# A hybrid SSD and stick-breaking trunk on one core: attention's products written in two parts, the output projection's units three steps earlier, and one sum of squares in PSUM

## The chip, the cores and the metric

The kernel runs on one core of one Trainium2 chip. The core's engines work side by side and meet over semaphores: PE (TensorE, matrix products), DVE (VectorE), ACT (ScalarE), POOL (GpSimd) and SP (SyncE, which here only issues transfers; ACT issues some too). Matmuls read SBUF and write PSUM, which the kernel divides into eight banks of 512 floats a partition. Each engine's instructions run in the order in which they stand, and so do the transfers that one engine issues: an instruction that waits holds all that stand behind it on its engine.

The metric is the device time of one execution in microseconds. Before the change it is 2861.54 us, the median of 3 runs (2855.9 to 2861.61).

## The reference

A trunk of two layers over 1040 tokens (16 learned ones and 1024 from the input), model width 1024, all in float32. Layer 0 is a Mamba-2 mixer and a gated FFN with a causal convolution; layer 1 is stick-breaking attention and such an FFN; RMSNorm stands before each. The parts that the change touches:

```python
def _rmsnorm(x, g):
    y = x * lax.rsqrt(jnp.mean(x * x, axis=-1, keepdims=True) + NORM_EPS)
    return y * g

def _stick_breaking_attention(q, k, v):            # per block of queries
    logits = jnp.einsum('bthd,bshd->bhts', q, k) * scale
    log_keep = jnp.where(visible, jax.nn.log_sigmoid(-logits), 0.0)
    later = lax.cumsum(log_keep, axis=3, reverse=True) - log_keep
    log_w = jnp.where(visible, jax.nn.log_sigmoid(logits) + later, -jnp.inf)
    return jnp.einsum('bhts,bshd->bthd', jnp.exp(log_w), v)

o = _stick_breaking_attention(q, k_shared, v_shared)   # 16 heads of 64
h = h + o @ sb_w_o[j]
h = h + _conv_ffn(_rmsnorm(h, ffn_norm), ...)
```

## The kernel before, in words

**Products.** A float32 product is made of three matmuls on rounded parts: each operand is split into a high part (a copy, by ACT) and a low part (the operand less its high part, by DVE or POOL), and `mm3` (L206 to L211) issues high by high (L209), high weight by low data (L210) and low weight by high data (L211). Where both parts of an operand come from, and when, is what the change moves.

**Attention** (`attention`, L1714). Heads go in 8 pairs. A pair has 18 steps: `i` runs over 9 blocks of 116 queries (the last has 112), `jj` over the thirds of the keys (348, 348, 344) that a block can see, from its own backwards. A step calls `weigh` (logits `lg` on PE, L1651; two sigmoids on ACT, L1652 and L1653; masks on POOL, L1657; two scans and a product on DVE, L1662 and L1663), then `place` and a piece of some projection (`pj` on PE), and `flush(LAG)`, which handles the step two back: `turn` transposes its weights on PE (L1685, `wT`) and ACT copies them out (`wt`, L1691); when a visit's blocks are all there (visits are blocks 0 to 2, 3 to 5, 6 and 7, and 8) the next `flush` calls `values`, PE's products with v (L1708, `po`, one PSUM bank), which ACT copies to `o` (L1710). After blocks 2, 5 and 8 an ACT transfer stores a third of the pair's `o` in DRAM (`o_d`, L1712).

The order of PE, DVE, ACT and POOL in this stage is the order of the program text; the transfers on SP and all other stages are placed by a scheduler.

**The output projection.** In pairs 0 to 6 PE's spare room in a step goes to projections of the next pair; in the last pair it goes to units of `o @ w_o` for pairs 0 to 3 (`o_blocks`, L1805), a generator that is advanced once in each step from `BEHIND` on, twice in each of the four turns of the loop behind the steps (the drain), and to its end in `o_proj`. A unit is 12 matmuls (4 pairs by 3) for 128 rows of output by 256 or 258 tokens, and an add to `h` on DVE (`accumulate`, L528 to L538); there are 8 x 4 of them. Its inputs are fetched by `fetch_o` (one float32 row of 514 or 512 tokens), split by `split_o` (ACT L1802, DVE L1803), and met by weights, which `parts` splits (ACT L1820, POOL through L102). Units write to the pool `mm`, which has two PSUM banks; the logits have two more (`lg2`), the transposes three (`sm`), `po` one (`ex`). Before, the generator's stages are: step 9 loads, steps 10 and 11 split the first two tiles, step 12 is the first unit, step 17 the sixth. Eight more units run in the drain and 18 behind it. Pairs 4 to 7 follow in `o_proj` and `enter_ffn`, with weights `w` from `load_wd`, tile by tile (four tiles of 256 or 258 tokens).

**The norm of the FFN.** Behind the last unit of a row of a tile, `square_row` (L1058) has ACT square it (L1061). For tile 0 (`m` = 8) DVE adds the eight squares up in a running sum (L1063, both operands in SBUF) and one matmul with ones sums over the partitions (L1041); for the other tiles each row has a matmul (L1067). This happens in both layers.

Of the kernel before, what the change touches and what calls it, by code (L numbers as in the profile page):

```python
# [13 lines left out]
P = 128  # L14
# [48 lines left out]
NPOOL = 3  # L63
DT0 = 0
LAG = 2
BEHIND = 9
VISITS = (0, 1, 2), (3, 4, 5), (6, 7), (8,)

NW = 8
# [36 lines left out]
class Trunk:  # L106
# [950 lines left out]

    def square_row(self, ms, h, f, s0, n, m):  # L1058

        q = self.tmp("sq")[:, :n]  # L1060
        self.nc.scalar.activation(q, h[f][:, HB + s0 : HB + s0 + n], AF.Square)  # L1061
        if f % m:
            self.nc.vector.tensor_tensor(self.squares, self.squares, q, op=ALU.add)  # L1063
# [629 lines left out]
    def values(self, p, visit, wt, v, o, od):  # L1693


        nc = self.nc
        first, last = visit[0], visit[-1]
        j, c0 = first // 3, first % 3 * CB
        end = CH[last][0] + CH[last][1]
        n = end - CH[first][0]  # L1700
        each = wt[0][0].shape[1]
        po = self.ex("po")
        order = [*range(first, last + 1), *range(first - 1, -1, -1)]
        for x, c in enumerate(order):
            t0 = max(c - first, 0) * CB
            q, r = divmod(c, each)
            for a in range(2):
                nc.tensor.matmul(po[64 * a : 64 * a + 64, t0:n], v[: CH[c][1], c, 64 * a : 64 * a + 64], wt[a][q][: CH[c][1], r, t0:n],  # L1708
                                 start=x == 0, stop=x == last, skip_group_check=True)
        nc.scalar.activation(o[:, c0 : c0 + n], po[:, :n], AF.Copy)  # L1710
        if last % 3 == 2:
            nc.scalar.dma_start(od[p, :, TT[j][0] : end], o[:, : TT[j][1]])  # L1712

    def attention(self, u, pool, hd):  # L1714


        od = self.dp.tile([PAIRS, P, L], F32, tag="o_d", name="o_d")
# [7 lines left out]
        pairs = [self.heads(u, p, pool) for p in range(PAIRS)]  # L1725
        turns, ready, wts, os, late, chores = [], [], {}, {}, [], []
        behind = self.o_blocks(hd, od)

        def flush(n):
            while ready:  # L1730
                p, visit = ready.pop()
                if visit[0] % 3 == 0:
                    os[p] = self.tmp("o")
# [21 lines left out]
        for p in range(PAIRS):  # L1755
            prev = None
            for n, (i, jj) in enumerate(steps):
# [22 lines left out]
                        chores += pair.load(loads[own, n])  # L1780
                flush(LAG)
                turns.append((p, i, jj, bt))
        while turns or ready:
            next(behind)
            next(behind)
            flush(0)
        return od, behind

    def fetch_o(self, od, p, x):
# [6 lines left out]
        self.nc.sync.dma_start(lo.bitcast(F32), od[p, :, g.at + s0 : g.at + s0 + m])  # L1796
        return hi, lo

    def split_o(self, hl):

        hi, lo = hl
        self.nc.scalar.activation(hi, lo.bitcast(F32), AF.Copy)  # L1802
        self.nc.vector.tensor_tensor(lo, lo.bitcast(F32), hi.bitcast(F32), op=ALU.subtract)  # L1803

    def o_blocks(self, hd, od):  # L1805

# [20 lines left out]

        def unit(f, j):
            w = ws[f]
            self.accumulate(h, f, *g.span(j), lambda i, f: tuple(x[:, i * P : i * P + P] for x in w), rows[j // 2], HB, self.mm, g.part(j // 2)[0])  # L1830
# [24 lines left out]
        for hl in rows[1][2:]:  # L1855
            self.split_o(hl)
        unit(1, 1)
        fetch_w(2)
        fetch_h(2)
        yield  # L1860
        order = [(0, 2), (0, 3), (1, 2), (1, 3)] + [(f, j) for f in range(2, KD) for j in range(4)]
        for x, (f, j) in enumerate(order):
            if x % 4 == 2 and x // 4 + 2 < KD:
                parts(x // 4 + 2)
                if x // 4 + 3 < KD:
                    fetch_w(x // 4 + 3)
                    fetch_h(x // 4 + 3)
            unit(f, j)
            yield

    def o_proj(self, od, blocks, pool):


        a = self.a
        first = PAIRS // 2
        for _ in blocks:
            pass

        def part(p, x):
            hl = self.fetch_o(od, p, x)  # L1880
            self.split_o(hl)
            return hl

        ops = [part(p, 0) for p in range(first, PAIRS)]
        ws = [self.load_wd(a["w_o"][first + i], i < 2) for i in range(4)]
        second = [part(p, 1) for p in range(first, PAIRS)]
        return self.enter_ffn(1, self.ho, [(ws, lambda: ops), (ws, lambda: second)], pool)


# [173 lines left out]
```

## Time and profile before

| | |
|---|---|
| median of 3 timed runs | 2861.54 us |
| profiled execution | 2864.79 us |
| its span, first to last instruction | 2862.9 us |
| mean granted TensorE clock | 0.996 |
| instructions | 56393 |
| attention, pairs 0 to 6 (span's clock) | about 1560 to 2006 us |
| last pair and drain | about 2006 to 2078 us |
| tile 0's squares in layer 1 | 2111 to 2124 us |

An execution has the name of its engine, line, operation and tiles in every row, and times count from the span's start. "x24" is 24 instructions, and an arrow in brackets names how long the engine stood idle before the row and what ended it. In rows of windows, each engine's busy time within the window is followed by its instructions, then come the clock granted to PE (1.00 is full), the busy share of the 16 transfer engines and their rate.

### The profile page before, as it was taken

The page shows a single profiled execution, that of the slowest core. Times are in us where ns is not written, and L with a number is a line of the kernel's source. Part 1 is how long each engine was busy: PE and PEld are TensorE (multiplying, and loading weights), DVE is VectorE, ACT ScalarE, POOL GpSimd, SP SyncE. Part 2 cuts the span into 40 slices and gives each one's busy share as a digit, 9 for nine tenths or more (in the row PEclk, how much of TensorE's full clock was granted, in tenths as well). Part 3 has the DMA queues.
Part 4 walks back from the last instruction along what each step waited for, and adds up shares of the span by engine and source line. Part 5 has one row for each costly group of instructions (what it writes and reads, how often), then busy time and mean ns, then how long its engine had stood idle before and what let it go on. Part 6 is the DMA issues. An engine that isn't in the chain of part 4 may idle for free.

```text
span 2862.9 us, 56393 instructions
## 1 busy us (share of the span) xinstructions
PE 2813.9 (98%) x21251; PEld 2695.1 (94%) x21251; DVE 2073.6 (72%) x3920; ACT 1589.3 (56%) x3093; POOL 1577.6 (55%) x2144
## 2 busy tenths in 40 slices
PE   8999999999999999999999999999899999999998
PEld 7989999999999999999999999999799999999888
DVE  5676666668597666677886888878669776766776
ACT  5555454543265656555335777777636555555433
POOL 2366455643529888868853111122254888885881
PEclk9999999999999999999999999999999999999999
DMA  4343334333413222245132222221432222225331
GB/s 119 88 112 103 107 86 134 108 132 101 126 59 97 81 79 79 80 156 174 43 128 77 66 69 62 63 59 47 136 107 76 80 80 78 81 82 184 111 104 67
DMA packets 136237, 273.32 MB, mean 95 GB/s; under 512 B 15924, under 2 KB 68285, under 8 KB 135965
## 3 DMA queue, kind: packets, MB, share of 16 engines
q1 hardware_dynamic: 130340, 258.55, 28.9%
q0 software_dynamic: 2048, 6.49, 0.6%
q10 hardware_dynamic: 3576, 4.67, 0.5%
q8 instruction: 168, 2.75, 0.4%
q14 instruction: 105, 0.85, 0.1%
HBM read 203.58 MB, written 51.16 MB: 89 GB/s over the span
## 4 chain that ended last, share of the span: by engine, by line
PE 89%; DVE 5%; ACT 2%; issue 2%; POOL 1%; DMA 0%; DVEq 0%; SPq 0%; ACTq 0%; POOLq 0%
PE p L211 10%; PE p L209 10%; PE p L210 10%; PE acc L209 8%; PE acc L211 8%; PE acc L210 8%; PE pj L209 8%; PE pj L210 7%; PE pj L211 7%; PE po L1708 2%; PE lg L1651 2%; PE wT L1685 2%; PE y L810 1%; PE S L799 1%; PE y L812 1%
## 5 line engine op out<-in xcount | busy, mean ns | idle before, releaser
L102 POOL TENSOR_TENSOR wl<-w,wh 128x256 fp32r<-128x256 f32 x760 | 678.9, 923 | 359.8 <-ACT wh L196 216.8
L209 PE MATMUL pj<-uh,wh 128*128 128x348 f32 (+2 forms) x1536 | 500.7, 327 | 2.1 <-DVE xbc L339 1.4
L210 PE MATMUL pj<-ul,wh 128*128 128x348 f32 (+2 forms) x1536 | 494.8, 322 | 0.8 <-DVE ul L320 0.8
L211 PE MATMUL pj<-uh,wl 128*128 128x348 f32 (+2 forms) x1536 | 492.1, 320 | 0.0
L209 PE MATMUL p<-bh,fh 128*128 128x262 f32 (+1 forms) x1408 | 400.8, 285 | 3.9 <-DVE p L1235 3.7
L211 PE MATMUL p<-bh,fl 128*128 128x262 f32 (+1 forms) x1408 | 400.8, 285 | 2.0 <-POOL fl L102 2.0
L210 PE MATMUL p<-bl,fh 128*128 128x262 f32 (+1 forms) x1408 | 397.5, 283 | 0.0
L102 POOL TENSOR_TENSOR fl<-x,fh 128x256 fp32r<-128x256 f32 x352 | 263.9, 782 | 190.3 <-ACT fh L1172 140.0
L210 PE MATMUL p<-bl,wh 128*128 128x262 f32 (+1 forms) x1040 | 295.5, 284 | 0.7 <-DVE bl L1096 0.7
L209 PE MATMUL p<-bh,wh 128*128 128x262 f32 (+1 forms) x1040 | 295.2, 284 | 0.8 <-ACT ft L1232 0.8
L211 PE MATMUL p<-bh,wl 128*128 128x262 f32 (+1 forms) x1040 | 294.3, 283 | 0.0
L209 PEld LDWEIGHTS pj<-uh,wh 128*128 128x128 f32 x1536 | 288.7, 188 | 4.5 <-ACT xbc L336 1.7
L210 PEld LDWEIGHTS pj<-ul,wh 128*128 128x128 f32 x1536 | 289.3, 188 | 2.4 <-DVE ul L320 1.4
L339 DVE SCALAR_TENSOR_TENSOR c<-p,params,c 128x260 f32<-128x260 f32 (+1 forms) x528 | 248.2, 479 | 57.5 <-ACT c L336 50.9
L211 PEld LDWEIGHTS pj<-uh,wl 128*128 128x128 f32 x1536 | 288.7, 188 | 0.1
L209 PEld LDWEIGHTS p<-bh,fh 128*128 128x128 f32 x1408 | 267.8, 190 | 4.8 <-DVE p L1235 4.1
L211 PEld LDWEIGHTS p<-bh,fl 128*128 128x128 f32 x1408 | 265.9, 189 | 2.9 <-POOL fl L102 2.7
L210 PEld LDWEIGHTS p<-bl,fh 128*128 128x128 f32 x1408 | 267.4, 190 | 0.1
L1232 ACT ACTIVATE ft<-p 128x262 f32<-128x262 f32 (+1 forms) x352 | 133.2, 382 | 178.9 <-DVE p L1235 110.9
L210 PE MATMUL acc<-gl,wh 128*128 128x260 f32 (+1 forms) x672 | 214.1, 320 | 0.0
L211 PE MATMUL acc<-gh,wl 128*128 128x260 f32 (+1 forms) x672 | 213.4, 320 | 0.0
L209 PE MATMUL acc<-gh,wh 128*128 128x260 f32 (+1 forms) x672 | 210.7, 320 | 0.1
(337 smaller groups left out, 7712.8 us busy)
## 6 DMA issues: line engine op xcount, KB each, us to landing
w<-in_w_up SPq DMA_DIRECT2D x88, 512.0 KB
w<-in_w_down SPq DMA_DIRECT2D x44, 512.0 KB
w<-in_w_in SPq DMA_DIRECT2D x40, 512.0 KB
E<-ea_d SPq DMA_DIRECT2D x32, 464.0 KB
D<-acs_d SPq DMA_DIRECT2D x32, 420.5 KB
g<-c SPq DMA_DIRECT2D x88, 130.0 KB
g<-c SPq DMA_DIRECT2D x88, 128.0 KB
b<-g SPq DMA_DIRECT2D x16, 520.0 KB
```

The source lines that it names most:

```text
L102: done.append(eng.tensor_tensor(out[:, c], x[:, c], y[:, c], op=op))
L209: self.behind(mm(out, wh, uh, start=first, stop=False, skip_group_check=joins), tie, "behind the sums of squares")
L210: mm(out, wh, ul, start=False, stop=False, skip_group_check=joins)
L211: self.last_mm = mm(out, wl, uh, start=False, stop=last, skip_group_check=joins)
L339: ins = nc.vector.scalar_tensor_tensor(out, ps[:, o + i : o + i + n], wcol(i), out, op0=ALU.mult, op1=ALU.add)
L799: nc.tensor.matmul(ps, bk[:n], xde[:n].rearrange("p h d -> p (h d)"), start=True, stop=True)
L810: nc.tensor.matmul(y, xdt[:n, i, :], dk[:, i, :], start=True, stop=c == 0)
L812: nc.tensor.matmul(y, state[:, i, :], ce[:, i, :], start=False, stop=True)
L1232: nc.scalar.activation(s[:, :N], ps[:, :N], AF.Copy)
L1651: nc.tensor.matmul(ps[:nt, a, :m], part[:, c0 : c0 + nt], ks[a][:, s0 : s0 + m], start=x == 0, stop=x == 1)
L1685: nc.tensor.transpose(pt[:ns, x * CB : x * CB + nt], bt[:nt, a, x * CB : x * CB + ns], self.ident[:nt, :nt])
L1708: nc.tensor.matmul(po[64 * a : 64 * a + 64, t0:n], v[: CH[c][1], c, 64 * a : 64 * a + 64], wt[a][q][: CH[c][1], r, t0:n], start=x == 0, st ...
```

## The change

`values` writes the products as two tiles, `hi` (ACT's copy, now rounded to the high part) and `lo` (a new DVE subtract, L1714 in the changed text, from the same PSUM bank). Both are stored, in a DRAM tile twice as large: high parts by ACT's queue as before, low parts by SP's. `fetch_o` loads both parts with one transfer, so `split_o` is gone (16 copies on ACT, 16 subtracts on DVE). The generator starts at step 5 (`BEHIND`): loads in step 5, weight parts in steps 6 and 7, `h` in step 8, and a unit in each step from 9 on; nine units are done by step 17, and 15 are left behind the drain. Weight blocks are fetched and split one block further ahead. The first two units in the drain take the two banks that the logits had, all others `mm`. For tile 0 of the norm the running sum lies in a PSUM tile of `sm`; the eighth add writes an SBUF tile for the matmul.

```diff
-BEHIND = 9
+BEHIND = 5
...
     def square_row(self, ms, h, f, s0, n, m):
-        q = self.tmp("sq")[:, :n]
+        q = self.sm("sq")[:, :n] if m > 1 and f == 0 else self.tmp("sq")[:, :n]
         self.nc.scalar.activation(q, h[f][:, HB + s0 : HB + s0 + n], AF.Square)
-        if f % m:
-            self.nc.vector.tensor_tensor(self.squares, self.squares, q, op=ALU.add)
-        elif m > 1:
+        if m > 1:
+            if f:
+                out = q if f == m - 1 else self.squares
+                self.nc.vector.tensor_tensor(out, self.squares, q, op=ALU.add)
+                q = out
             self.squares = q
...
-        nc.scalar.activation(o[:, c0 : c0 + n], po[:, :n], AF.Copy)
+        hi, lo = (x[:, c0 : c0 + n] for x in o)
+        nc.scalar.activation(hi.bitcast(F32R), po[:, :n], AF.Copy)
+        nc.vector.tensor_tensor(lo.bitcast(F32R), po[:, :n], hi, op=ALU.subtract)
         if last % 3 == 2:
-            nc.scalar.dma_start(od[p, :, TT[j][0] : end], o[:, : TT[j][1]])
+            for x, (q, t) in enumerate(zip((nc.scalar, nc.sync), o)):
+                q.dma_start(od[p, x, :, TT[j][0] : end], t[:, : TT[j][1]])
...
+        both = self.lg2("acc")
+        banks = iter([lambda s, a=a: both[:, a] for a in range(2)])
+        self.unit_bank = lambda s: next(banks, self.mm)(s)
         while turns or ready:
...
-        hi, lo = t[:, :m], t[:, QW // 2 : QW // 2 + m]
-        self.nc.sync.dma_start(lo.bitcast(F32), od[p, :, g.at + s0 : g.at + s0 + m])
-        return hi, lo
-    def split_o(self, hl):
-        hi, lo = hl
-        self.nc.scalar.activation(hi, lo.bitcast(F32), AF.Copy)
-        self.nc.vector.tensor_tensor(lo, lo.bitcast(F32), hi.bitcast(F32), op=ALU.subtract)
+        both = t.rearrange("p (y c) -> p y c", y=2)[:, :, :m]
+        self.nc.sync.dma_start(both.bitcast(F32), od[p, :, :, g.at + s0 : g.at + s0 + m].rearrange("y p c -> p y c"))
+        return both[:, 0], both[:, 1]
...
         fetch_w(1)
         yield
-        for hl in rows[0][:2]:
-            self.split_o(hl)
-        yield
-        for hl in rows[0][2:]:
-            self.split_o(hl)
         parts(0)
         yield
-        rows[1] = [self.fetch_o(od, p, 1) for p in range(K)]
+        parts(1)
+        fetch_w(2)
+        yield
         fetch_h(0)
         fetch_h(1)
+        yield
+        rows[1] = [self.fetch_o(od, p, 1) for p in range(K)]
+        fetch_h(2)
         unit(0, 0)
         yield
-        parts(1)
         unit(0, 1)
         yield
-        for hl in rows[1][:2]:
-            self.split_o(hl)
         unit(1, 0)
         yield
-        for hl in rows[1][2:]:
-            self.split_o(hl)
         unit(1, 1)
-        fetch_w(2)
-        fetch_h(2)
+        parts(2)
+        fetch_w(3)
+        fetch_h(3)
```

In what follows each row is a place in an engine's order: its line, operation, written tile, read tiles and shape. The line numbers of the changed text are two to five higher than before.

On PE, the last pair's step 9 as it was (logits 116 wide, a projection's half `pj`, then at once step 10's transposes):

```order
L1651 MATMUL lg_24943<-k_23929,qs_24791 116x116 x2
L1616 MATMUL pv_24957<-ident,v_24900 116x128 x3
L209 MATMUL pj_24925<-uh_17766,wh_24228 128x344
L210 MATMUL pj_24925<-ul_17767,wh_24228 128x344
L211 MATMUL pj_24925<-uh_17766,wl_24229 128x344
L209 MATMUL pj_24925<-uh_17768,wh_24228 128x344
L210 MATMUL pj_24925<-ul_17769,wh_24228 128x344
L211 MATMUL pj_24925<-uh_17768,wl_24229 128x344
L1685 MATMUL wT_24980<-ident,bt_24839 116x116 x3
```

And now: the first unit's 12 matmuls (five are shown) stand between that half and step 10's transposes.

```order
L211 MATMUL pj_25022<-uh_17768,wl_24292 128x344
L209 MATMUL acc_25079<-o_24898,wh_24939 128x258
L210 MATMUL acc_25079<-o_24898,wh_24939 128x258
L211 MATMUL acc_25079<-o_24898,wl_24940 128x258
L209 MATMUL acc_25079<-o_24900,wh_24939 128x258
L210 MATMUL acc_25079<-o_24900,wh_24939 128x258
```

On DVE, steps 10 to 12 of the last pair as they were, with scans and product of each step and four splits:

```order
L1662 SCALAR_TENSOR_TENSOR kp_24990<-kp_24990,kp_24940,one 116x349 x2
L1663 TENSOR_TENSOR bt_24991<-bt_24991,kp_24990 116x2x348
L1803 TENSOR_TENSOR o_24968<-o_24968 128x514
L1803 TENSOR_TENSOR o_24970<-o_24970 128x514
L1662 SCALAR_TENSOR_TENSOR kp_25023<-kp_25023,kp_24990,one 116x349 x2
L1663 TENSOR_TENSOR bt_25024<-bt_25024,kp_25023 116x2x348
L1803 TENSOR_TENSOR o_24972<-o_24972 128x514
L1803 TENSOR_TENSOR o_24974<-o_24974 128x514
L1662 SCALAR_TENSOR_TENSOR kp_25063<-kp_25063,one 116x233 x2
```

And now: the splits' places hold the units' adds, and the new subtract (`o` from `po`) stands behind step 12's product, ahead of step 13's scans.

```order
L538 TENSOR_TENSOR h_25029<-h_25029,acc_25079 128x258
L1664 SCALAR_TENSOR_TENSOR kp_25103<-kp_25103,kp_25041,one 116x349 x2
L1665 TENSOR_TENSOR bt_25104<-bt_25104,kp_25103 116x2x348
L538 TENSOR_TENSOR h_25029<-h_25029,acc_25122 128x256
L1664 SCALAR_TENSOR_TENSOR kp_25146<-kp_25146,kp_25103,one 116x349 x2
L1665 TENSOR_TENSOR bt_25147<-bt_25147,kp_25146 116x2x348
L538 TENSOR_TENSOR h_25031<-h_25031,acc_25167 128x258
L1664 SCALAR_TENSOR_TENSOR kp_25191<-kp_25191,one 116x233 x2
L1665 TENSOR_TENSOR bt_25192<-bt_25192,kp_25191 116x2x232
L538 TENSOR_TENSOR h_25031<-h_25031,acc_25208 128x256
L1714 TENSOR_TENSOR o_25232<-po_25233,o_25231 128x348
L1664 SCALAR_TENSOR_TENSOR kp_25260<-kp_25260,kp_25191,one 116x349 x2
```

On SP's queue, around the last pair's loads of o, now: a low part's store (L1717) stands ahead of them and another behind, and the last loads of queries (`qs`), which stood ahead of the loads of o before, stand behind the first four.

```order
L1592 DMA k_23988<-klo_24763 64x344
L1717 DMA o_d<-o_24653 128x344
L1805 DMA o_24898<-o_d 128x2x514
L1805 DMA o_24900<-o_d 128x2x514
L1805 DMA o_24902<-o_d 128x2x514
L1805 DMA o_24904<-o_d 128x2x514
L1607 DMA qs_24859<-qs_24859 64x2x344
L1607 DMA qs_24861<-qs_24861 64x2x344
L1717 DMA o_d<-o_24945 128x348
L1818 DMA w_3489_25227<-in_w_o_f 128x512
L1829 DMA h_25029<-h_d 128x1026
```

More of the change, by code (lines that the diff above doesn't have):

```diff
@@ L1727, in attention @@
         behind = self.o_blocks(hd, od)
+        self.unit_bank = self.mm
         def flush(n):
@@ L1829, in unit @@
             w = ws[f]
-            self.accumulate(h, f, *g.span(j), lambda i, f: tuple(x[:, i * P : i * P + P] for x in w), rows[j // 2], HB, self.mm, g.part(j // 2)[0])
+            self.accumulate(h, f, *g.span(j), lambda i, f: tuple(x[:, i * P : i * P + P] for x in w), rows[j // 2], HB, self.unit_bank, g.part(j // 2)[0])
         rows[0] = [self.fetch_o(od, p, 0) for p in range(K)]
@@ L1875, in o_proj @@
         first = PAIRS // 2
+        self.unit_bank = self.mm
         for _ in blocks:
             pass
[L1879 to L1884, printed above, removed]
+        ops = [self.fetch_o(od, p, 0) for p in range(first, PAIRS)]
         ws = [self.load_wd(a["w_o"][first + i], i < 2) for i in range(4)]
-        second = [part(p, 1) for p in range(first, PAIRS)]
+        second = [self.fetch_o(od, p, 1) for p in range(first, PAIRS)]
         return self.enter_ffn(1, self.ho, [(ws, lambda: ops), (ws, lambda: second)], pool)
```

14 lines of the change are left out of this document (7 added, 7 removed).

## The prediction

> **What bounds the kernel now.** I read the page first: which engine is full, and what the chain that ended last is made of.
>
> ```profile
> PE 2813.9 (98%) x21251; PEld 2695.1 (94%) x21251; DVE 2073.6 (72%) x3920; ACT 1589.3 (56%) x3093; POOL 1577.6 (55%) x2144
> PE 89%; DVE 5%; ACT 2%; issue 2%; POOL 1%; DMA 0%; DVEq 0%; SPq 0%; ACTq 0%; POOLq 0%
> ```
>
> TensorE (PE) is busy for 98% of the span and carries 89% of the chain. The change leaves its matmuls alone (as many rows on PE as before), so it can win only where PE stands still, or runs at a lower clock, and can lose only by making PE wait. So I read PE's waits next, in the whole execution.
>
> ```profile
> PE acc L209 <- DVE h L538: 5.6, 2, 4.0
> PE lg L1651 <- ACT bt L1653: 4.9, 13, 0.8
> PE acc L210 <- DVE o L1803: 3.0, 2, 2.0
> PE acc L209 <- ACT wh L1820: 1.2, 1, 1.2
> ```
>
> The columns are microseconds in total, times, longest. Lines 1, 3 and 4 all lie in the output projection: its units in the last pair, and the tiles behind them. Waits alone understate the loss, so the third view is windows by stage: pairs 0 to 6; the last pair up to its step 9; steps 9 to 17; the start of the drain; the drain and the projection's rest; then tile 0's squares.
>
> ```profile
> core 0: us, PE busy (x) PEld busy (x) DVE busy (x) ACT busy (x) POOL busy (x), PEclk, DMA share, GB/s
> 1563.00:2006.00 443.00, 440.38 (x3371) 408.67 (x3367) 371.28 (x646) 336.74 (x805) 86.52 (x248) 1.00 0.23 62
> 2006.00:2020.00 14.00, 12.64 (x89) 10.88 (x87) 11.04 (x15) 12.09 (x27) 2.08 (x8) 1.00 0.42 116
> 2020.00:2057.00 37.00, 30.68 (x199) 25.01 (x199) 29.55 (x43) 24.06 (x51) 9.52 (x18) 0.91 0.33 111
> 2057.00:2062.00 5.00, 3.42 (x30) 3.21 (x29) 3.83 (x6) 1.66 (x4) 2.05 (x2) 1.00 0.02 5
> 2062.00:2112.00 50.00, 50.00 (x448) 48.61 (x447) 18.10 (x39) 18.73 (x35) 25.99 (x37) 1.00 0.53 177
> 2118.00:2122.00 4.00, 0.30 (x3) 0.09 (x1) 3.69 (x5) 0.00 (x0) 2.01 (x3) 0.87 0.00 0
> 2122.00:2128.00 6.00, 5.72 (x24) 5.44 (x24) 3.17 (x9) 3.20 (x6) 0.50 (x1) 0.52 0.67 217
> 2033.00:2040.00 7.00, 7.00 (x32) 3.67 (x32) 2.38 (x5) 0.33 (x1) 0.42 (x2) 0.57 0.50 183
> ```
>
> Two places are loose. In 2020 to 2057 PE is idle for 37.00 - 30.68 = 6.3 us and its clock is 0.91; the last row shows where: seven microseconds at 0.57. In 2118 to 2128 it stands for nearly 4 us and then runs at 0.52. Around them it is full: 440.38 of 443 in pairs 0 to 6, all of 2062 to 2112.
>
> **Term A: steps 9 to 17 of the last pair and the start of the drain.** These are PE's rows with their waits:
>
> ```profile
> 2019.74 0.62 PE L1651 MATMUL lg<-k,qs 128*116 128x116 f32 x4 [0.37 <-ACT bt L1653]
> 2027.81 0.68 PE L1651 MATMUL lg<-k,qs 128*116 128x232 f32 x4 [0.78 <-ACT bt L1653]
> 2029.71 0.39 PE L209 MATMUL acc<-o,wh 128*128 128x258 f32 x1 [1.22 <-ACT wh L1820]
> 2030.74 0.28 PE L209 MATMUL acc<-o,wh 128*128 128x258 f32 x1
> 2032.40 0.58 PE L210 MATMUL acc<-o,wh 128*128 128x258 f32 x1 [1.01 <-DVE o L1803]
> 2053.32 0.39 PE L210 MATMUL acc<-o,wh 128*128 128x256 f32 x1 [2.04 <-DVE o L1803]
> 2057.45 0.36 PE L209 MATMUL acc<-o,wh 128*128 128x256 f32 x1
> 2060.68 0.39 PE L209 MATMUL acc<-o,wh 128*128 128x256 f32 x1 [1.58 <-DVE h L538]
> ```
>
> Before, `split_o` turns the loaded output into high and low parts on ACT and DVE in these very steps, and the units wait for it (the two that name `o`; the 1.22 is for a copy of weights that stands behind the same splits on ACT). The change makes both parts in `values` and loads them, so the splits go. Their size, beside what DVE does in each step:
>
> ```profile
> L1802 ACT ACTIVATE o<-o x16: 626/632/674, 2024.4 to 2092.0; 128x514 fp32r<-128x514 f32 x8, 128x512 fp32r<-128x512 f32 x8
> L1803 DVE TENSOR_TENSOR o<-o 128x514 fp32r<-128x514 f32 x4 | 3.3, 862 | 0.0
> L1803 DVE TENSOR_TENSOR o<-o 128x512 fp32r<-128x512 f32 x4 | 2.8, 728 | 0.0
> L1662 DVE TENSOR_TENSOR_SCAN kp<-kp,kp,one 116x349 f32<-116x349 f32 x110 | 97.7, 929 | 25.3 <-ACT kp L1652 25.1
> L1663 DVE TENSOR_TENSOR bt<-bt,kp 116x696 f32<-116x696 f32 x70 | 62.4, 892 | 9.2 <-ACT wt L1691 0.5
> ```
>
> Eight of the sixteen splits lie in these steps: 3.3 + 2.8 = 6.1 us of DVE and 8 x 0.63 = 5.1 of ACT. The units now begin at step 9 instead of 12, their weight parts are made in steps 6, 7 and 12, one block further ahead, and the first two units of the drain go to the logits' two banks, so that the add of the unit before (the last row, 1.58) need not come first.
>
> What could be won: 6.3 us of idle, 1.6 in the drain, and 37 x 0.09 = 3.3 us of slow clock, together 11.2. A wait also costs a refill: the matmul after it occupies 0.39 instead of 0.28, ten times about 0.1, so some 12. What stays: the logits' wait for ACT (a part of the 0.78), and two new costs. First, ACT copies weights in steps 6 and 7, where it is already full: 12.09 of 14 us in the second window; two copies of about 0.65 (the size of a split, 0.63) put it later, and PE's logits wait for ACT there. I count 0.5 to 1.3 lost. Second, DVE. Of its 29.55 us in the stretch 6.1 go, three more adds (0.41 each) and one new subtract (0.51, row below) come, and 25.2 remain. PE's own work there is 37 - 12 = 25 us. The two are level, so DVE's scans can set the pace for a while; a step's two scans, product and add are 2 x 0.93 + 0.89 + 0.41 = 3.2, a little less where they overlap. I take 0.5 us for it, 0 to 3 as bounds. **A = 12 - 0.5 - 0.9 - 0.5, about -10 us** (-7 to -12).
>
> Does the slow clock go with the waits? The 0.57 window has PE busy throughout; before it lies a stretch in which PE is idle for half the time, no single wait above 1.22. The Trainium skill, "TensorE: Matmul & The Clock Gate" (Part 1, the HAM clock gate), has the clock halve after an idle window of about 3.4 us; the fall after 2118 to 2122 agrees, the one at 2033 does not by single waits, so here it is the share of idle time that counts. Read by that rule alone, a cold clock after short waits would have another cause and stay: A would be 3 less, an estimate.
>
> **Term B: tile 0's squares.** PE's rows, and DVE's and POOL's at that time:
>
> ```profile
> 2122.28 0.58 PE L209 MATMUL acc<-o,w 128*128 128x256 f32 x1 [3.98 <-DVE h L538]
> 2122.66 0.42 PE L210 MATMUL acc<-o,w 128*128 128x256 f32 x1
> 2122.87 0.41 PE L211 MATMUL acc<-o,w 128*128 128x256 f32 x1
> 2111.41 10.47 DVE L1063 TENSOR_TENSOR sq<-sq,sq 128x258 f32<-128x258 f32 x4
> 2114.42 5.59 POOL L102 TENSOR_TENSOR fl<-x,fh 128x256 fp32r<-128x256 f32 x8
> L1063 DVE TENSOR_TENSOR sq<-sq,sq x14: 420/433/8879, 780.2 to 2124.0; 128x260 f32<-128x260 f32 x7, 128x258 f32<-128x258 f32 x7
> L538 DVE TENSOR_TENSOR h<-h,acc x192: 404/420/519, 681.4 to 2854.0; 128x256 f32<-128x256 f32 x72, 128x260 f32<-128x260 f32 x56, 128x348 f32<-128x348 f32 x32, 128x344 f32<-128x344 f32 x16
> ```
>
> One add of two SBUF tiles, normally 433 ns, took 8879 while POOL subtracted back to back; the add of h stood behind it, and PE's bank behind that. The add of h itself has one operand in PSUM, and of 192 none took over 519 ns, though POOL works 55% of the time. With the running sum in PSUM the square adds have that form, so four of them take 4 x 0.42 = 1.7 instead of 10.47, and PE need not wait: 3.98 us. The clock loss goes too (matmuls start 0.21 apart there, 50 / 448 = 0.11 in the full stretch): 6 x (1 - 0.52) = 2.9. **B = -6.6 us**, a little under the sum because a short wait may stay; bounds -6.9 and 0 (the hold has another cause). Layer 0 has the same edit and no PE wait on these adds: 0.
>
> The Trainium skill, "SBUF — State Buffer" (SBUF: two separate sides), says that a DVE operation with two SBUF inputs and a GpSimd operation that reads SBUF exclude each other for a whole instruction. A POOL instruction here takes 5.59 / 8 = 0.70, so by the letter the add would be held 0.7 us, not 8.4: the trace shows a hold over a whole train. If so long a hold has a cause beyond those two inputs, the move to PSUM may not end it; that is the second rival.
>
> **Term C: pairs 0 to 7, and what is left.** Each pair gets four new subtracts on DVE and three low stores on SP's queue. A subtract of 348 columns from PSUM is nearest to the second row here (the first is PE's only wait in pairs 0 to 6):
>
> ```profile
> PE lg L1651 <- ACT bt L1653: 2.6, 7, 0.7
> L538 DVE TENSOR_TENSOR h<-h,acc 128x348 f32<-128x348 f32 x32 | 16.3, 513 | 21.9 <-PE acc L211 21.6
> 2011.19 1.34 SPq L1605 DMA_DIRECT2D qs<-qs  x2
> 2014.32 6.13 SPq L1796 DMA_DIRECT2D o<-o_d  x8
> 2022.00:2024.00 2.00, 2.00 (x17) 1.98 (x16) 1.86 (x5) 1.83 (x4) 0.67 (x3) 1.00 1.01 362
> ```
>
> 0.51 twice, and by width about 0.4 and 0.27: 1.7 us a pair. DVE works 371 of 443 us in these pairs, 84%, so there is room, and the subtract comes just after `values`, PE's longest piece of a step. Cover: PE's own matmuls. With that gone it would be 8 x 1.7 = 13.6 us. I take 0. The low store stands on SP behind the subtract and ahead of the loads of queries and keys for the next steps; qs is issued at 2011.19 for logits that start at 2019.74, some 7 us of slack after its transfer. The loads of o carry both parts, four of 514 KB for the first two tiles; at 362 GB/s that is 5.7 us. They are issued three steps earlier than before (2014.32) and their unit comes three steps earlier, so they keep a few us of slack: 0. Behind the drain two units instead of three now stand ahead of the first matmuls with w_o's second half, whose weights also wait for transfers: 0 to 1.5, I take 0.5. Smaller reorderings in the FFN's `up` (one group of its matmuls): 0, plus or minus 1. The other eight splits, after 2062, lay under a full PE: 0.
>
> **Sum:** -10 - 6.6 + 0.5 = about -16. The profiled execution took 2864.8 (span 2862.9); the median of the three timed runs is 2861.5, so I put the gain under that: 2861.5 - 16 = 2845.5.
>
> **Rivals.**
> 1. *A's wait only changes its name.* DVE and ACT are as full as PE in steps 9 to 17, and the doubled loads must land before step 9. If the units wait for either, PE idles in the same stretch and the clock falls again; half of A is left: -5 - 6.6 + 0.5 = -11, 2850.5. For it speaks 25.2 of DVE against 25 of PE; against it that PE runs two steps ahead of the scans.
> 2. *B fails.* The hold is not from the two SBUF inputs, or goes to the next DVE operation in line: -9.5, 2852. For it speaks only the length of the hold; against it the 192 adds of h.
> 3. *Slower: SP's queue.* The low store waits for DVE's subtract, which comes after ACT's copy and ahead of two scans; while it waits, no load behind it on SP is issued. From a slip of 7 us on, qs comes late and PE's logits wait. At 3 us in each of the eight pairs that is +24, 2869.5. For it: SP is one queue, in order. Against it: a subtract can be late by about one step (3 to 6 us), below the slack.
> 4. *1 and 2 together,* or DVE's 13.6 us in the open: about -4, 2857.5. The parts then do little.
>
> **How the numbers follow.** Chances: forecast 0.65, first rival 0.13, second 0.10, third 0.05, fourth 0.07. What this kernel's measurement can tell from no change is about 0.2%, 5.7 us. Forecast and the first two rivals are faster by more than that: 0.88; the fourth is the same: 0.07; the third slower: 0.05. The forecast's own range is 2840 to 2851 from the bounds of A (-7 to -12), B and C; taking in the first two rivals with the same spread it becomes 2838 to 2856.
>
> **What would show it.** A: in the stretch that was 2020 to 2062, PE idle under 2 us and a clock of 1.00, no wait of `acc` on `o`; the stretch from step 9's logits (2019.74) to the drain's start (2057.45) about 29 us instead of 37.7, with nine units in it instead of six. B: the square adds at 0.42 us each and no 3.98 us wait; matmuls 0.11 to 0.12 apart where they were 0.21. C: PE's waits in pairs 0 to 6 as before, 2.6 us in all. It is wrong if pairs 0 to 6 take over 3 us longer, if the clock in the last pair stays at 0.91, or if a square add still takes microseconds.

## The result, and the profile after

The changed kernel takes 2853.73 us (median of 22 runs, 2852.82 to 2860.24), the kernel before 2858.61 (22 runs, 2855.74 to 2866.63). The ratio is 0.9984, with a 95% interval of 0.9977 to 0.9990: 0.16% faster, a gain of some 5 us where 16 were forecast. The time lies inside the wider of the two predicted ranges (2838 to 2856), above the forecast's own (2840 to 2851); under a third of the forecast gain came. The timings fall into groups: 11 of the 22 before lie at 2855.7 to 2857.9 and 10 at 2861.4 and more, while after the change 19 lie at 2852.8 to 2855.3 and 3 at 2859.7 to 2860.2, so that between the lower groups alone the gain is 3.4 us.

The profiled executions differ by more: 2864.79 before, 2855.13 after, spans of 2862.9 and 2853.3 us. Where the 9.6 us between them come from can be read off. First PE's waits in the whole execution, after the change (microseconds in total, times, longest):

```profile
PE lg L1653 <- ACT bt L1655: 6.3, 11, 0.8
PE acc L209 <- DVE h L538: 4.3, 2, 3.3
PE wT L1687 <- DVE v L1620: 1.8, 4, 1.0
```

The wait for `o` is gone (3.0 before), the one for `wh` too (1.2). The wait for the add of `h`, 5.6 before, is still 4.3, and the logits' wait for ACT has grown from 4.9 to 6.3; the transposes' wait for DVE's product of v (third row) was 1.0. Then the windows, with the columns of those before:

```profile
2020.00:2057.00 37.00, 34.88 (x272) 31.79 (x271) 31.92 (x46) 26.66 (x55) 12.29 (x26) 1.00 0.56 192
2057.00:2062.00 5.00, 1.69 (x10) 1.48 (x10) 3.84 (x5) 0.33 (x1) 2.16 (x2) 0.81 0.26 77
2062.00:2066.00 4.00, 4.00 (x24) 3.18 (x24) 0.42 (x1) 0.00 (x0) 0.00 (x0) 0.50 1.00 375
2066.00:2070.00 4.00, 4.00 (x36) 2.99 (x33) 0.40 (x1) 1.27 (x5) 0.00 (x0) 0.89 1.01 385
2118.00:2122.00 4.00, 4.00 (x31) 3.84 (x30) 1.37 (x4) 3.08 (x7) 3.31 (x6) 1.00 0.29 104
```

In 2020 to 2057 things are as hoped: 2.1 us of idle instead of 6.3, a clock of 1.00 instead of 0.91, 272 matmuls instead of 199. (Step 9 starts at 2024.46 here and at 2019.74 before; from its logits to the drain's first unit PE idles 1.0 us instead of 6.3.) The squares are, too: PE is busy throughout 2118 to 2122. But a new hole stands at 2057.7 to 2061.0, ahead of the drain's second unit, with the clock at 0.50 behind it. PE's rows there in the timeline (start, length, engine, line, operation; in brackets the idle time before and what ended it):

```profile
2056.03 0.36 PE L209 MATMUL acc<-o,wh 128*128 128x256 f32 x1
2057.44 0.28 PE L211 MATMUL acc<-o,wl 128*128 128x256 f32 x1
2061.03 0.58 PE L209 MATMUL acc<-o,wh 128*128 128x256 f32 x1 [3.31 <-DVE h L538]
2061.41 0.41 PE L210 MATMUL acc<-o,wh 128*128 128x256 f32 x1
2061.62 0.41 PE L211 MATMUL acc<-o,wl 128*128 128x256 f32 x1
```

and DVE's:

```profile
2056.52 0.42 DVE L538 TENSOR_TENSOR h<-h,acc 128x256 f32<-128x256 f32 x1
2056.85 2.20 DVE L1664 TENSOR_TENSOR_SCAN kp<-kp,kp,one 112x349 f32<-112x349 f32 x2
2059.18 1.12 DVE L1665 TENSOR_TENSOR bt<-bt,kp 112x696 f32<-112x696 f32 x1
2060.23 0.74 DVE L538 TENSOR_TENSOR h<-h,acc 128x258 f32<-128x258 f32 x2
```

The first unit of the drain ends at 2057.7. The second starts when both adds of the last row are done, at 2060.97: the second of those two adds is that of the first unit, which wrote the other bank. Both units write halves of one two-bank tile, and the program has the second wait for the reader of the first (experiment 3 puts this to the test). That add stands behind step 17's scans and product, which DVE reaches late.

The other place is pairs 0 to 6. Here are the timeline's first logits rows of pair 0 and of pair 7, first of the kernel before, then of the changed one:

```profile
1538.02 0.60 PE L1651 MATMUL lg<-k,qs 128*116 128x116 f32 x4
1989.02 0.59 PE L1651 MATMUL lg<-k,qs 128*116 128x116 f32 x4
```

```profile
1538.83 0.60 PE L1653 MATMUL lg<-k,qs 128*116 128x116 f32 x4
1993.33 0.59 PE L1653 MATMUL lg<-k,qs 128*116 128x116 f32 x4
```

451.0 us became 454.5. (So pairs 0 to 6 of the kernel before run from 1538 to 1989 us, not from 1560 to 2006 as the table ahead has it, and the prediction's window of 2006 to 2020 holds steps 4 to 8 of the last pair.) Step by step, every pair is level with before up to step 10 and then drops back by 0.1 to 0.8 us in steps 11 and 12. In pair 2 the changed kernel's timeline looks like this on DVE:

```profile
1697.27 1.39 DVE L1555 SCALAR_TENSOR_TENSOR wl<-w,params,wh 128x128 fp32r<-128x128 f32 x4
1698.58 0.50 DVE L1714 TENSOR_TENSOR o<-po,o 128x348 fp32r<-128x348 f32 x1
1699.01 1.64 DVE L1664 TENSOR_TENSOR_SCAN kp<-kp,one 116x349 f32<-116x349 f32 x2
...
1707.13 0.51 DVE L1577 TENSOR_TENSOR k<-pj,r 128x348 f32<-128x348 f32 x1
```

then on ACT and on PE, and last the same logits in the kernel before:

```profile
1707.67 0.50 ACT L1588 ACTIVATE k<-k 128x348 fp32r<-128x348 f32 x1 [1.21 <-DVE k L1577]
1711.54 0.68 PE L1653 MATMUL lg<-k,qs 128*116 128x232 f32 x4 [0.62 <-ACT bt L1655]
```

```profile
1709.07 0.69 PE L1651 MATMUL lg<-k,qs 128*116 128x232 f32 x4 [0.28 <-ACT bt L1653]
```

The new subtract of the first visit falls into a stretch in which DVE hardly rests (scans, splits of the next pair's weights). All behind it slips by its 0.43 us and a little more; ACT idles 1.21 us for the key product (0.38 before), everything behind that copy on ACT is late, and PE's logits of step 12 wait 0.62 us, where before they waited 0.28.

In sum, in us and against before: pairs 0 to 6 +3.5, start of the last pair +0.4, step 9 to the drain's first unit -10.4 (31.6 instead of 37.7, with three more units of 1.44), the drain to the last products +4.4 (24.6 instead of 20.2), the rest of the projection with the squares -6.7 (39.2 instead of 50.2, less the three units that now come earlier), what follows the squares -1.6, what lies ahead of attention +0.8: together -9.6. The last two are in part what single executions differ by: against the three other executions of the kernel before (experiments 5, 6 and 12) the -1.6 would be -0.5 to -0.8, and attention starts at 1538.0 in one execution of that kernel and at 1539.1 in another.

### The profile page after: what moved, and what is told of

Read it like the earlier page. It is cut to its first block, busy times and chain, and to the rows that moved or that the text cites. A ratio compares the mean times of both kernels' runs of the same rounds, so it can differ in the third digit from the quotient of the medians.

```text
span 2853.3 us, 56464 instructions
## 1 busy us (share of the span) xinstructions
PE 2809.2 (98%) x21251; PEld 2691.9 (94%) x21251; DVE 2065.4 (72%) x3936; ACT 1580.2 (55%) x3077; POOL 1578.6 (55%) x2144
## 4 chain that ended last, share of the span: by engine, by line
PE 91%; DVE 4%; ACT 2%; POOL 1%; issue 1%; DMA 0%; SPq 0%; ACTq 0%; DVEq 0%; POOLq 0%
PE p L209 10%; PE p L210 10%; PE p L211 10%; PE acc L209 8%; PE acc L211 8%; PE acc L210 8%; PE pj L209 8%; PE pj L210 8%; PE pj L211 8%; PE po L1710 3%; PE lg L1653 2%; PE wT L1687 2%; PE y L810 1%; PE S L799 1%; PE y L812 1%; PE ms L1069 1%
```

## The experiments

All are compared with the kernel before, by ratio with its 95% interval; the changed kernel's is 0.9984 [0.9977, 0.9990].

**1. Before, with the squares alone.**

```diff
-        q = self.tmp("sq")[:, :n]
+        q = self.sm("sq")[:, :n] if m > 1 and f == 0 else self.tmp("sq")[:, :n]
...
+                out = q if f == m - 1 else self.squares
```

> The kernel before, with only the third part of the change: tile 0's running sum of squares in PSUM. Theory (the hold of DVE's add of two SBUF tiles costs PE 3.98 us and 2.9 us of clock): the profile loses about 6.6 us between 2111 and 2128, no square add over 0.5 us. The 22 timings of before stand in two groups, near 2856 and near 2861.5, 5.5 us apart; if that is the hold falling into some executions only, the timings here stand in one group at or below 2856, and the median gains 2 to 5 us. Rival (the hold has another cause): the add of h or the next DVE operation is held instead, profile and times as before, within 1 us.

Ratio 0.9993 [0.9983, 1.0003]; 11 runs, five at 2855.9 to 2858.2 and six at 2860.7 to 2862.1. In the profile (2856.86) the 3.98 us wait is gone and no square add is over 438 ns (the tile's groups: shortest, median, longest in ns, then the first and last start):

```profile
L1065 DVE TENSOR_TENSOR sq<-sq,sq x14: 426/435/438, 780.4 to 2116.2; 128x260 f32<-128x260 f32 x7, 128x258 f32<-128x258 f32 x7
```

From the first logits to the squares' matmul it took 582.7 us instead of 589.8. So the mechanism holds in the profile, and yet the timings stand in the same two groups as before's. What makes the groups is not (only) this hold.

**2. The changed kernel with the sum in SBUF** (the edit of experiment 1 taken back).

> The changed kernel with tile 0's squares back in SBUF. Theory: the parts are additive, so the profile is about 6.6 us longer than the changed kernel's in that place if the hold occurs (2860), and the timings have two groups again, 5 to 6 us apart, the lower at 2853. Rival (the units' new schedule has moved POOL's subtractions away from the squares, so that nothing is held): same as the changed kernel, 2853 to 2854, within 1 us.

Ratio 0.9985 [0.9976, 0.9994], 2859.26 in the median, 2853.2 to 2862.7. The profiled execution (2857.01) held no square add for long: 430 to 934 ns, and no wait of PE there. From its timeline, DVE's first four square adds and two of POOL's instructions beside them:

```profile
2110.13 3.21 DVE L1063 TENSOR_TENSOR sq<-sq,sq 128x258 f32<-128x258 f32 x4
2112.13 1.80 POOL L102 TENSOR_TENSOR f<-w,f 128x256 fp32r<-128x256 f32 x2
```

DVE's four adds take about 0.8 each, where one alone takes 0.43, and POOL's instructions beside them 0.92 each, where those behind the adds take 0.73: both slow a little. Before, DVE's one add took 8.88 us and POOL's instructions beside it stood 0.70 apart. With adds in SBUF and the new order, PE lost nothing in this execution: from the first logits to the squares' matmul 580.9 us, and 581.0 with PSUM. Nothing was held, as the rival said, but not for its reason: POOL still works beside the squares.

**3. One bank of the logits for the drain.**

```diff
-        banks = iter([lambda s, a=a: both[:, a] for a in range(2)])
+        banks = iter([lambda s: both[:, 0]])
```

> The changed kernel, but only the first unit of the drain takes a bank of the logits, the second takes mm. Theory (the two logits' banks are one tile, so the second unit waits for the add of the first, which stands on DVE behind the last scans; 3.31 us of wait and half clock after it): the wait goes, since mm's next bank was released earlier, and the time falls 5 to 6 us against the changed kernel, to about 2848. Rival (DVE is simply behind, so PE waits for the next add instead, whichever bank it uses): the wait moves to the next unit or to the products behind it, and the time changes by less than 1.5 us.

2848.43 us, ratio 0.9955 [0.9943, 0.9968]: 5.3 us below the changed kernel by the medians, as the theory said; by the profiles 6.2 us from the first logits to the squares' matmul (574.8 against 581.0). The hole is gone in PE's timeline, and in the windows the clock stays at 1.00:

```profile
2052.72 0.39 PE L209 MATMUL acc<-o,wh 128*128 128x258 f32 x1 [1.00 <-DVE h L538]
2057.85 3.16 PE L1710 MATMUL po<-wt,v 116*64 116x232 f32 x32
```

```profile
2057.00:2062.00 5.00, 5.00 (x50) 3.90 (x50) 3.36 (x6) 0.89 (x4) 1.36 (x2) 1.00 0.52 166
2062.00:2066.00 4.00, 4.00 (x37) 4.00 (x37) 0.85 (x2) 1.45 (x5) 0.00 (x0) 1.00 0.99 339
```

The second unit takes mm's next bank, whose add was done before; the products start straight behind it. DVE is as late as before, so it was not its lateness as such that PE paid for, but the tile: the rival falls. What stays of DVE's lateness is the 1.00 us at step 17's unit.

**4. The first visit's subtract later.**

```diff
-        nc.vector.tensor_tensor(lo.bitcast(F32R), po[:, :n], hi, op=ALU.subtract)
+        def low():
+            nc.vector.tensor_tensor(lo.bitcast(F32R), po[:, :n], hi, op=ALU.subtract)
...
+        if first == 0:
+            self.low = low
+        else:
+            low()
...
+                if n == 11:
+                    self.low()
                 bt = self.weigh(i, jj, now[0].qd[i // 3], now[0].ks, prev, pool)
```

> The changed kernel, but in each pair the new subtract of the first visit (348 columns) and its store stand on DVE ahead of step 11's scans instead of step 8's. Theory (DVE has no idle time from step 5 to 12, so the subtract there delays the key projection's product, ACT's copy behind it, and step 12's logits by 0.4 to 0.8 us in each pair): pairs 0 to 6 get back 2.5 to 3.5 us, PE's waits there fall from 5.3 to about 2.7. Rival (the slip comes from the scans, which run slower beside the larger traffic, not from the subtract's place): within 1 us of the changed kernel.

Ratio 0.9983 [0.9974, 0.9992], no different from the changed kernel by time. In the profile pairs 0 to 6 take 452.9 us, 1.6 less than the change's 454.5, where the theory had 2.5 to 3.5, and 1.9 more than before's 451.0. The logits' waits for ACT there fall to 3.0 us (4.5 in the changed kernel, 2.6 before). Counted from each pair's first logits to its last, the slip against before falls from 3.5 us in all to 0.5: so the subtract's place is what made steps 11 and 12 late. But now each next pair starts 0.2 us late, 1.3 in all, where the changed kernel loses nothing. The subtract's time has moved there: in step 17 DVE comes to the key product later, and ACT's copy of it, which stands ahead of the two sigmoids that read the logits, waits longer. In pair 3, first of the changed kernel, then of this one:

```profile
1794.78 0.49 ACT L1588 ACTIVATE k<-k 128x348 fp32r<-128x348 f32 x1 [0.63 <-DVE k L1577]
```

```profile
1799.29 0.50 ACT L1588 ACTIVATE k<-k 128x348 fp32r<-128x348 f32 x1 [1.00 <-DVE k L1577]
```

The next pair's logits, which use the same banks, start right behind the second sigmoid. So all but 0.5 of the 3.5 us is the subtract; a later place alone gets back 1.6.

**5, 6 and 12. The kernel before, three more profiles.**

> The kernel before, unchanged, for a second profile. Theory (the long hold of DVE's add of two SBUF tiles is an event of single executions, since with the squares in SBUF again the second experiment's longest square add took 0.93 us): the hold of 8.9 us at tile 0's squares is absent or elsewhere, PE's wait of 3.98 us with it, and another such hold may stand at another add of two SBUF tiles. Rival (the hold belongs to this order of instructions and comes each time): a square add of 8 to 9 us and a wait of 4.0 us again.

> The kernel before, unchanged, for a third profile: as the second. If the hold is an event of single executions, the long square add is absent in at least one of the two.

> The kernel before, unchanged, for a profile of its faster group (2856), which the first three profiles (2862.6 to 2864.8) were not. Theory: if this execution takes about 2856, the hold of 8.9 us at the squares is absent, which makes it the difference between the groups; if it takes 2862 or more, the hold is there again.

They took 2862.63, 2863.89 and 2862.34 us. In the first two the hold is there again, 8.87 and 8.97 us, with the wait of 4.0 and 4.1 us: with the first profile, three of three, which spoke for the rival. The fourth decides against it. Its square adds in the timeline:

```profile
2116.72 3.28 DVE L1063 TENSOR_TENSOR sq<-sq,sq 128x258 f32<-128x258 f32 x4
```

No hold and no wait of PE; but another one, 1240 us earlier, in layer 0's `up`, where an add of two SBUF tiles took 5.57 us while POOL worked back to back, and PE stood and ran on at a lower clock (DVE's and PE's timeline, then a window):

```profile
875.89 5.57 DVE L1235 TENSOR_TENSOR ft<-ft,ft 128x262 f32<-128x262 f32 x1
882.43 0.39 PE L209 MATMUL p<-bh,wh 128*128 128x262 f32 x1 [3.89 <-ACT ft L1232]
```

```profile
880.00:885.00 5.00, 2.57 (x15) 2.57 (x16) 4.05 (x8) 2.88 (x6) 1.17 (x2) 0.85 0.25 94
```

Attention starts 5.5 us later in this execution. The same program has one hold or the other, and each is worth about 6 us. The profiles of the other kernels fit: those of experiments 4, 7, 8 and 9, which lie in the upper group of their kernel's timings, have the hold at 876 us, and those of the changed kernel and of experiments 1, 2, 3, 10 and 11, which do not, have neither hold. An execution of the kernel before in its group at 2856, which by this would have neither, was not profiled.

**7. Parts made in the attention, but the units' old schedule.** (BEHIND 9, stages and weight blocks as before without the splits, all units in mm.)

```diff
-BEHIND = 5
+BEHIND = 9
...
-        both = self.lg2("acc")
...
         fetch_w(1)
         yield
+        yield
         parts(0)
         yield
-        parts(1)
-        fetch_w(2)
-        yield
+        rows[1] = [self.fetch_o(od, p, 1) for p in range(K)]
         fetch_h(0)
         fetch_h(1)
-        yield
-        rows[1] = [self.fetch_o(od, p, 1) for p in range(K)]
-        fetch_h(2)
         unit(0, 0)
         yield
+        parts(1)
         unit(0, 1)
...
```

> The changed kernel with the generator's stages as before (units from step 12, loads in step 9, all units in mm): parts made in the attention, no splits, squares in PSUM. Theory: the splits alone made the units wait, so the waits of 1.01, 2.04 and most of 1.22 us go and the clock holds; the add in front of the drain's second unit is still behind the last scans, 1.6 to 2.5 us; the pairs lose 3.5 us as in the changed kernel. From step 9's logits to the last logits some 8 us less than before, so by time 2851 to 2854, about as the changed kernel or below it. Rival (earlier units are what fills PE): PE has too little work in steps 9 to 11, the stretch gains under 4 us, and the time is 2856 or more.

2853.30 us, ratio 0.9976 [0.9965, 0.9987], with most runs at 2853 as for the changed kernel. Its profile (2859.75) has the hold at 876 us. From step 9's logits to the drain's first unit it takes 29.95 us with six units, 7.75 less than before, at a clock of 1.00 throughout; the drain's wait is the old one:

```profile
2030.06 0.62 PE L1653 MATMUL lg<-k,qs 128*116 128x116 f32 x4 [0.37 <-ACT bt L1655]
2060.01 0.39 PE L209 MATMUL acc<-o,wh 128*128 128x256 f32 x1 [0.29 <-DVE h L538]
2063.28 0.39 PE L209 MATMUL acc<-o,wh 128*128 128x256 f32 x1 [1.60 <-DVE h L538]
```

So three quarters of the stretch's gain (7.75 of 10.4) come from making the parts in attention. The earlier units give the other 2.7 us, and the drain's second bank took more than that back: up to the squares' matmul this kernel is 2.1 us ahead of the changed one (578.9 against 581.0).

**8. One bank and the later subtract together** (the edits of experiments 3 and 4).

> The changed kernel with both mends: one logits' bank in the drain, and the first visit's subtract at step 11. Theory (the two are independent): the pairs get back 1.6 us as in the fourth experiment beside the 5.3 us of the third, so about 2846 to 2847 in its fast group. Rival (the later subtract makes DVE later at the drain's start): no gain over the third experiment, 2848 or more.

2849.37 us, ratio 0.9956 [0.9942, 0.9969], three runs at 2848.0 to 2849.4 and two at 2853. From the first logits to the squares' matmul 573.7 us, against 574.8 in experiment 3: one microsecond less, where the theory had 1.6; by time (2849.37 against 2848.43) no gain can be told. The profiled execution (2852.93) has the hold at 876 us, ahead of that stretch.

**9. PSUM sum in layer 1 alone.**

```diff
     def enter_ffn(self, layer, h, last, pool):
+        self.sum_in_psum = layer == 1
...
-        q = self.sm("sq")[:, :n] if m > 1 and f == 0 else self.tmp("sq")[:, :n]
+        q = self.sm("sq")[:, :n] if m > 1 and f == 0 and self.sum_in_psum else self.tmp("sq")[:, :n]
```

> The changed kernel with the running sum in PSUM in layer 1 alone; layer 0 adds in SBUF as before. In the slower profiles of kernels with PSUM sums in both layers (experiments 4, 7 and 8) an add of two SBUF tiles in layer 0's up is held for 5.6 us at 875 us and all that follows starts 5.8 us later; with SBUF sums in layer 0 (before, three profiles, and experiment 2) that hold was never seen, but one at 894 us that cost nothing. Theory (the PSUM sum in layer 0 moves DVE against POOL so that this hold can fall where it delays PE): the timings stand in one group, at 2853 to 2855, without the 2859 to 2860 ones. Rival (any kernel has it in some executions): two groups again, 6 us apart.

2860.03 us, ratio 0.9985 [0.9975, 0.9995], four runs at 2855.0 to 2856.7 and seven at 2859.6 to 2862.2, the profile with a hold of 5.57 us at 876. The theory falls: layer 0's sum does not bring that hold about. Experiment 12, on the kernel before, says the same.

**10 and 11. Versions with all mends:** one bank, the later subtract, the sum in PSUM in layer 1; in the second also the weight blocks' splits at another place:

```diff
-            if x % 4 == 2 and x // 4 + 3 < KD:
-                parts(x // 4 + 3)
-                if x // 4 + 4 < KD:
-                    fetch_w(x // 4 + 4)
-                    fetch_h(x // 4 + 4)
+            if x % 4 == 1 and x > 4 and x // 4 + 2 < KD:
+                parts(x // 4 + 2)
+                if x // 4 + 3 < KD:
+                    fetch_w(x // 4 + 3)
+                    fetch_h(x // 4 + 3)
```

> One logits' bank in the drain, the first visit's subtract at step 11, PSUM sum in layer 1 alone. Theory: the gains of experiments 3 and 4 and one group of timings: 2846 to 2849, none above 2851. Rival (the hold at 875 us has nothing to do with layer 0's sum): as experiment 8, 2848 to 2853.5 in two groups.

> As experiment 10, and from the drain on the weight blocks are split one unit earlier than before the change instead of a block ahead, so that POOL's subtractions of blocks 3 and 4 no longer stand beside the scans of steps 15 and 16. Theory (POOL's subtractions slow DVE's scans: 2.68 us for two at 2049.9, 2.20 at 2056.9, against 1.78): DVE is 1 to 1.5 us less behind at step 17, the unit's wait of about 1 us for h goes, and the time is 1 us below experiment 10. Rival (POOL's work then falls beside step 17's scans, and the block's weights come late for the fourth unit of the drain): no gain, or 1 to 2 us slower.

The first takes 2851.73 us (six runs, 2846.4 to 2854.7, two groups again), ratio 0.9956 [0.9941, 0.9971]. The second takes 2847.66 (five runs, 2845.8 to 2848.9), ratio 0.9944 [0.9928, 0.9959], the lowest of all. Its wait of 1.00 us for step 17's unit is gone: DVE's two scans of step 15 take 1.63 us, with POOL's subtractions no longer beside them, where they took 2.68 in the changed kernel and in experiment 10.

```profile
2047.65 1.63 DVE L1665 TENSOR_TENSOR_SCAN kp<-kp,one 112x345 f32<-112x345 f32 x2
2053.55 2.21 DVE L1665 TENSOR_TENSOR_SCAN kp<-kp,kp,one 112x349 f32<-112x349 f32 x2
```

```profile
2020.00:2057.00 37.00, 36.11 (x291) 32.92 (x290) 32.37 (x47) 24.27 (x50) 10.60 (x22) 1.00 0.45 162
```

PE is idle for 0.9 us in the window, after 6.3 before and 2.1 in the changed kernel. Step 17's scans still take 2.21 (second row; 2.20 in the changed kernel), but PE does not wait behind them. By the profiles of the two (2846.40 and 2845.80) the last edit is worth 0.6 us, one execution of each. The first one's three runs above 2853 lie about 6 us over its others, the size of a hold; none of the three was profiled, so that is argued and not shown.

## Why the prediction was wrong, point by point

Of the 16 us forecast 4.9 came. 6.0 are missing in the drain, 3.5 in pairs 0 to 6, and 4.7 because B's stall and the execution that the sum was made against do not stand for the median; some 3 more than forecast came elsewhere.

- **A, the stretch from step 9 on: right, and somewhat low.** The waits on `o` and `wh` went, the clock held at 1.00 with them. In experiment 7, where of the work in these steps only the splits go and the units keep their old places, it holds too: the slow clock went with the splits' waits. ACT's copies of weights, 0.9 in the sum, cost 0.4, by the logits' wait ahead of step 9. The gain to the drain's first unit was 10.4 us, where the sum had 8.4 (10 less the drain's 1.6). (The predicted length of "about 29 us instead of 37.7, with nine units in it" was an error of my sum: it left out the three added units, 4.3 us; it took 31.6. The same slip made PE's work of 25 us there look level with DVE's 25.2; with the three units it is some 29.)
- **A, the drain: the step that failed.** That "the first two units of the drain go to the logits' two banks, so that the add of the unit before (the last row, 1.58) need not come first" is true of the first unit alone. The second shares its tile with the first and waits for that one's add, behind step 17's scans: 3.31 us of wait, and 2.9 more by the clock (0.50 from the unit's start at 2061.0 to 2066, 0.89 to 2070). Forecast -1.6, measured +4.4. Experiment 3 removes just this and gains 5.3 us by time, 6.2 by the profiles. This could be seen beforehand in the program: the two banks are one tile, `both`, and one tile has one order of writers and readers.
- **DVE's pace** was given 0.5 us with bounds 0 to 3. In steps 9 to 17 it cost the 0.99 us wait at step 17; DVE's lateness is also why the add of the drain's first unit came so late.
- **B, the squares: the mechanism right, its weight wrong.** Where the hold falls it costs what was forecast: 6.7 us. In the nine profiles with layer 1's sum in PSUM no square add of tile 0 there took over 435 ns; in the five with it in SBUF three have the hold, and in the other two the adds take up to 784. But one profile was taken for all executions. In the fourth profile of before the hold is absent, and in the timings of experiment 1 the gain is 0.07% with an interval that contains none.
- **C, pairs 0 to 6: mis-sized.** I took 0 because DVE works 84% there; it cost 3.5 us, which is past the 3 that the prediction named as a sign of being wrong. The average covers steps 0 to 4, where DVE idles 8.7 us (pair 3, before), and steps 5 to 17, where it idles 1.9 in all, 0.1 to 0.2 a step. All but 0.5 us is the first visit's subtract in the second stretch (experiment 4); the cause of the 0.5 is open. The rival on SP's queue did not come: no logits waited for a transfer in these pairs. The 0.5 us for the weights of the second half did not come either: in 2062 to 2112 PE is never idle.
- **The base.** The sum was made against an execution of 2864.79 that stood 6.2 us over its kernel's median; the three timings shown put the median at 2861.5, 22 put it at 2858.6. The profiles differ by 9.6 us and the medians by 4.9. Against the forecast's 16 us the profiles lost 6.0 in the drain and 3.5 in pairs 0 to 6, and gained 2.0 more in the stretch and about 1 elsewhere; what B then adds is seen only against executions with the hold. Experiment 1's execution, which has B alone and no hold, shows what the other terms are worth together: 582.7 us from the first logits to the squares' matmul against 581.0, a gain of 1.7 where the sum had 9.5. That the time still fell into the wider range is therefore no success of A: most of the profiles' 9.6 us, 7.1 by the same count, is the hold.
- **The rivals.** By the profiles the first (half of A, PE waiting in the same stretch for DVE) came nearest: A was 6.0 instead of 10. It had the engine and the size, but not the reason, one tile for two banks. By the medians the gain of 4.9 lies nearest to the fourth's 4, half of A with no B; of its two causes only the first holds, since B's mechanism works wherever the hold falls.

## What to carry to other kernels

Two banks that belong to one tile are one resource to the program's ordering: before counting on both, look who releases the second. Read an engine's room from the steps in which the new work falls, not from its share over the stage. And before a long stall in one profile is booked as a gain, profile the same kernel again: a stall that other executions lack is paid back only in part.

## What the runs showed of the hardware

DVE's adds of two SBUF tiles meet POOL's back-to-back work in two ways, in executions of the same program. Either both slow a little (experiment 12: 0.63 to 0.78 us for a square add of 0.43, and 0.92 for POOL instructions of 0.73), or one add stands until POOL's row of instructions ends, 5.6 us at 876 or 8.9 us at 2111, with POOL's instructions 0.70 apart as elsewhere. The Trainium skill, "SBUF — State Buffer" (SBUF: two separate sides), describes an exclusive lock held for an instruction. Neither form is quite that: in the mild one an add and a POOL instruction pass every 0.88 us, less than 0.43 and 0.70 one behind the other, and the long one outlasts a dozen POOL instructions. What picks between them in an execution was not found. Adds with one operand in PSUM were never held: 438 ns at most in all of tile 0's square adds of experiment 1.

TensorE's clock fell to 0.50 in a single idle time of 3.3 us (2057.7 to 2061.0) and was full again by 2067; with a wait of 1.0 us alone (experiment 3) it did not fall. Before the change it also fell at 2032, behind seven microseconds (2026 to 2033) in which PE was busy for 3.7 and no single wait was over 1.22 us. Each of these falls, and the one at 2121 before, lasted 6.8 us (2060.1 to 2066.9; 2032.2 to 2039.1; 2121.0 to 2127.8).
